# Reordering the result's stores, and two instructions late in the attention, in a two-layer encoder on one core

## The chip, the cores and the metric

The kernel runs on one core of a Trainium2 chip. The metric is the time of one execution on the device in microseconds (us); lower is better. A core has TensorE (PE, the matrix engine, with weight loads shown apart as PEld), VectorE (DVE), ScalarE (ACT), GpSimd (POOL) and SyncE (SP), each with its own stream of instructions that runs in order. They meet through semaphores. DMA engines move data between the chip's memory and the on-chip buffers; a transfer is issued by an instruction in the stream of SP, ACT or POOL, and such a stream is called that engine's queue here.

## The reference

One sequence of 512 tokens with 1024 features passes through two layers; all inputs are float32. Cut to what matters:

```python
def stick_breaking_attention(h, w_qkv, w_o):      # layer 0's mixer, 16 heads of 64
    ...
        z = jnp.einsum('bhqd,bhkd->bhqk', qb, kb).astype(jnp.float32) * scale
        mask = k_pos < q_pos
        log_keep = jnp.where(mask, jax.nn.log_sigmoid(-z), 0.0)
        after = lax.cumsum(log_keep, axis=3, reverse=True) - log_keep
        w = jnp.where(mask, jnp.exp(jax.nn.log_sigmoid(z) + after), 0.0)
        outs.append(jnp.einsum('bhqk,bhkd->bhqd', w.astype(vb.dtype), vb))
    ...
    return o @ w_o

def reference(...):
    for layer in range(DEPTH):                     # 2
        h = rms_norm(x, norm_mix[layer])
        y = stick_breaking_attention(...) if layer % 2 == 0 else rglru_block(...)
        x = x + y
        h = rms_norm(x, norm_mlp[layer])
        x = x + squared_relu_mlp(h, mlp_w1[layer], mlp_w2[layer])
    return rms_norm(x, norm_final)
```

The weight of a key for a query is sigmoid(z) times the product of sigmoid(-z) over the keys between the two. `rglru_block` is a gated linear recurrence over time, `squared_relu_mlp` is relu(h @ w1) squared, times w2, with 4096 inner features.

## The kernel before, in words

**Numbers in two halves.** A float32 operand is split into a rounded high half and the rest, the low half. ScalarE makes the high half (a cast), VectorE subtracts it for the low half, and a product is three matmuls: high x high, high x low, low x high (`three`, lines 234 to 238). Nearly all of the work of VectorE and ScalarE is this splitting. Weights come as slabs of 1024 x 128; `slab` (line 219) issues the load on SP's queue (line 223), casts the slab on ScalarE (line 229) and subtracts on VectorE (line 231), in one or more cuts. It takes its raw tile from a ring of 3 and its halves from rings of 4, so an early slab has to be used up before a later one is split.

**Who orders what.** TensorE's instructions run in the order in which the program emits them. For the other engines a planner simulates the program and picks, for each engine, the next instruction that is ready by its own clock, the earlier emitted one first, unless something holds it: `tc.issue_after(ins)` puts the instructions of a block behind `ins` on its engine, `tc.high_priority()` puts them first, and an `Ordered` wrapper (line 788) chains every instruction of one engine to the one before. An instruction that was emitted late can thus be planned early. What the planner chose is fixed; on the chip an engine whose next instruction isn't ready waits, and everything behind it waits too.

**The attention** (lines 303 to 770) works on 8 pairs of heads. A pair has a chain of 8 score steps (`score_steps`, line 586; 2 heads j times 4 query blocks qb of 128) and a chain of 18 value steps (`value_steps`, line 628). A score step multiplies queries and keys into one of two PSUM banks with the tag z (lines 595 and 596). ScalarE reads the bank twice: line 603 makes sigmoid(z) into `w`, line 604 sigmoid(-z) into `keep`; after the second read the bank is free. GpSimd masks the diagonal block (line 608), VectorE runs the product over the keys as a recurrence, `tensor_tensor_scan` (line 614), and GpSimd multiplies (line 618). A value step transposes the weights of one key block kb on TensorE (line 636) and splits the result (high half line 651, low half line 652), then multiplies it with the values (lines 662 and 663). For the last key block, kb = 3, the halves are 128 columns in tiles named `lasth` and `lastl`.

The chains are interleaved with filling matrix products by due times (constants SCORE0, PACE and so on), so that TensorE always has work. Late in the attention, the filling work is the output projection: `so_part` for output slabs 4 and 5, `so_steps` for slabs 0 to 3 (line 537), and `so_late`. Two chains overlap at that point: the scores of the last pair, 7 (PAIRS - 1), and the values of pair 6 (PAIRS - 2). The scores of pair 7, head 1, block 2 stand at about 202 us in TensorE's stream; the values of pair 6, head 1, kb = 3 at about 205 to 209 us.

**After the attention** come the residual with the first feed-forward layer, the recurrent block, and the second feed-forward layer. The feed-forward layers multiply blocks of matrices with fewer block products (`Mlp`, from line 795), and their last products go with the final normalization.

**The end** (function `end` inside the last `with`, lines 1847 to 1880) has the result in row tiles t = 0 to 3 of 128 tokens and halves h = 0, 1 of 512 features, so `(t, h)` is a store of 128 x 512, 256 KB. A tile is squared and summed on ScalarE; `root` (line 1815) makes 1/rms; the tile is multiplied by the norm's gain and by 1/rms. `both` (line 1827) does the two multiplications in one VectorE instruction (line 1831); `one` (line 1835) only multiplies by 1/rms, on ScalarE (line 1840) or, for the very last piece, on VectorE (line 1842), where GpSimd has multiplied by the gain before. Each ends with `store` (line 1821), which issues the transfer on SP's queue. In program order the stores are (0,0), (0,1), (1,0), (1,1), (2,1), (2,0), right half of (3,0), (3,1), left half of (3,0); the halves of (3,0) are 128 KB each. GpSimd's instructions in this function are held to program order by `EG = Ordered(G)` (line 1779); SP's aren't.

Of the kernel before, what the change touches and what calls it, by code (L numbers as in the profile page):

```python
# [15 lines left out]
ALU = mybir.AluOpType  # L16
# [3 lines left out]
S = 512  # L20
D = 1024
C = D // P
# [15 lines left out]
CUT = 2  # L38
# [26 lines left out]
def hybrid_encoder(  # L65
# [23 lines left out]
    nc = tc.nc  # L89
    V, A, G, PE = nc.vector, nc.scalar, nc.gpsimd, nc.tensor  # L90
# [16 lines left out]
    def f(ap):  # L107
        return ap.bitcast(F32)
# [107 lines left out]
    slabs, loads = count(), count()  # L216
    behind = [None]

    def slab(src, cut=1, ks=range(C), at=0):
        raws = rawpools[next(loads) % len(rawpools)]  # L220
        raw = raws.tile([P, C, P], F32, tag="raw", name="raw", bufs=3 if raws is wpool else 1)
        k = slice(ks.start, ks.stop)
        nc.sync.dma_start(out=raw[:, k, :], in_=src[:, k, :])
        pool = wpools[next(slabs) % len(wpools)]
        wh = half_slab(pool, "wh", at)
        wl = half_slab(pool, "wl", at)
        for i in range(cut):
            k = slice(ks.start + i * len(ks) // cut, ks.start + (i + 1) * len(ks) // cut)
            A.copy(wh[:, k, :], raw[:, k, :])  # L229
            with tc.issue_after(behind[0]) if behind[0] else nullcontext():  # L230
                V.tensor_tensor(wl[:, k, :], raw[:, k, :], f(wh[:, k, :]), ALU.subtract)  # L231
        return wh, wl
# [63 lines left out]
    NB = S // P  # L296
# [10 lines left out]
    with ExitStack() as actx:  # L307
# [228 lines left out]

        def so_steps(c, tag):

            wh, wl = slab(w_so[c], CUT)
            ps = bank(tag)  # L540
            so[c] = ps, wh, wl
            for k in range(C - 2):
                three(ps, bh[:, k, :], bl[:, k, :], wh[:, k, :], wl[:, k, :], k == 0, False)
                yield
# [42 lines left out]
        def score_steps(pair):  # L587

            for j in range(2):
                for qb in range(NB):  # L590
                    n = (qb + 1) * P
                    nn = max(n, 2 * P)
                    lhsT = q[pair][j][:, qb * P : n]
                    z = bank("z")
                    PE.matmul(z[:, :nn], lhsT, kh[pair][j][:, :nn], start=True, stop=False)
                    PE.matmul(z[:, :nn], lhsT, kl[pair][j][:, :nn], start=False, stop=True)
                    keep = home_tile("keep", 4, "keep")
                    pool = home if qb == NB - 1 else hp
                    wt = pool.tile([P, n], F32, tag=f"w{qb}", name=f"w{qb}", bufs=3)
                    if pair == 0:  # L600
                        V.tensor_tensor(keep[:, :n], z[:, :n], norm["r"][:, :n], ALU.mult)
                        z = keep
                    A.activation(wt, z[:, :n], AF.Sigmoid, scale=norm["rp"][:, qb : qb + 1])
                    marks["keep"] = A.activation(  # L604
                        keep[:, :n], z[:, :n], AF.Sigmoid, scale=norm["rn"][:, qb : qb + 1]
                    )
                    t = wt[:, qb * P : n]
                    G.affine_select(
                        t, t, pattern=[[-1, P]], compare_op=ALU.is_gt,
                        fill=0.0, base=0, channel_multiplier=1,  # L610
                    )
                    sc = scans[turns[0] % 3]
                    turns[0] += 1
                    V.tensor_tensor_scan(  # L614
                        sc[:, S - n : S][:, ::-1], keep[:, :n][:, ::-1], later[:, S - n :][:, ::-1],
                        1.0, ALU.mult, ALU.max,
                    )
                    G.tensor_tensor(wt, wt, sc[:, S - n + 1 : S + 1], ALU.mult)  # L618
                    w[pair, j, qb] = wt
                    yield  # L620

        lows = []

        def low():
            pair, o = lows.pop()
# [2 lines left out]
        def value_steps(pair):  # L628
# [3 lines left out]
            def turn(j, kb):  # L632
# [17 lines left out]
                with tc.high_priority():  # L650
                    A.copy(dh, tr[:, :n])
                    left[j, kb] = V.tensor_tensor(dl, tr[:, :n], f(dh), ALU.subtract)

            def times(j, kb):
                nonlocal o
# [1105 lines left out]
    with ExitStack() as mctx:  # L1761
# [14 lines left out]
            mlp.turns = count(4)  # L1776

        gb = []
        EG = Ordered(G)

        def factors():
            for h in range(2):
# [35 lines left out]
            V.reciprocal(rt, rt)  # L1818
            return rt

        def store(t, h, cols=slice(0, S)):
            nc.sync.dma_start(
                out=out[t * P : (t + 1) * P, h * S + cols.start : h * S + cols.stop],
                in_=mlp.y(t, h)[:, cols],
            )
# [6 lines left out]
            store(t, h, cols)  # L1832
            return done

        def one(t, h, rt, cols=slice(0, S), e=A, last=None):

            y = mlp.y(t, h)[:, cols]
            if e is A:
                with tc.issue_after(last.ins) if last else nullcontext():
                    A.activation(y, y, AF.Copy, scale=rt)  # L1840
            else:
                V.tensor_scalar(y, y, rt, None, ALU.mult)
            store(t, h, cols)

        def end(ws, xs):
            EG.turn(True)
            for t in range(2):
                square(t, 0, 0)
                scaled(t, 0)
# [26 lines left out]
            both(2, 0, two, last=mlp.gained)  # L1876
            rt = root(3, 2)
            both(3, 0, rt, parts[1])
            one(3, 1, rt)
            one(3, 0, rt, parts[0], V)  # L1880

        end.ready = factors
# [69 lines left out]
```

## Time and profile before

| what | us |
|---|---|
| median of 3 runs | 1023.08 (1023.04 to 1023.11) |
| the profiled execution's own time | 1023.33 |
| its span, first to last instruction | 1021.0 |
| TensorE busy | 1012.2 |
| VectorE busy | 862.2 |
| ScalarE busy | 710.9 |
| GpSimd busy | 178.3 |

The profile is of one execution. Times in its rows are in us from the span's start unless marked ns. A row of the timeline has the start, the duration, the engine, the line of the program, the operation, the tile written and those read, and the shapes; `x2` means that two instructions were merged into the row, and a bracket at the end is idle time before it and what ended it. Matmuls overlap: a row's duration is longer than the distance to the next start, so distances between starts are what counts. A row of the waits has the engine and tile that waited, what it waited for, the total, the number of times and the longest. A row of the windows view has the stretch, its length and the busy time of PE, PEld, DVE, ACT and POOL with the number of instructions in brackets, then the granted TensorE clock, the share of the DMA engines and GB/s. A row of the DMA view has the tiles, the queue, the count, the size of one and the median time in us from issue to landing.

### The profile page before, as it was taken

The page shows a single profiled execution, that of the slowest core. Times are in us where ns is not written, and L with a number is a line of the kernel's source. Part 1 is how long each engine was busy: PE and PEld are TensorE (multiplying, and loading weights), DVE is VectorE, ACT ScalarE, POOL GpSimd, SP SyncE. Part 2 cuts the span into 40 slices and gives each one's busy share as a digit, 9 for nine tenths or more (in the row PEclk, how much of TensorE's full clock was granted, in tenths as well). Part 3 has the DMA queues.
Part 4 walks back from the last instruction along what each step waited for, and adds up shares of the span by engine and source line. Part 5 has one row for each costly group of instructions (what it writes and reads, how often), then busy time and mean ns, then how long its engine had stood idle before and what let it go on. Part 6 is the DMA issues. An engine that isn't in the chain of part 4 may idle for free.

```text
span 1021.0 us, 16117 instructions
## 1 busy us (share of the span) xinstructions
PE 1012.2 (99%) x5954; PEld 892.3 (87%) x5954; DVE 862.2 (84%) x1157; ACT 710.9 (70%) x1109; POOL 178.3 (17%) x243
## 2 busy tenths in 40 slices
PE   9999999999999999999999999999999999999997
PEld 7988888888888988988988888888988988988986
DVE  7978787847789898898899888985998898898897
ACT  7777676835766873873875799966973873873875
POOL 0454344420000010010011121100020010010013
PEclk9999999999999999999999999999999999999999
DMA  7845454537536767667683576452367667667653
GB/s 239 232 110 148 119 150 101 154 106 269 153 82 197 180 150 196 172 149 198 166 225 83 139 186 170 104 200 89 88 143 203 171 143 202 180 138 201 168 122 104
DMA packets 53550, 161.53 MB, mean 158 GB/s; under 512 B 6752, under 2 KB 8288, under 8 KB 53472
## 3 DMA queue, kind: packets, MB, share of 16 engines
q1 hardware_dynamic: 42240, 120.48, 35.9%
q0 software_dynamic: 10944, 39.85, 22.8%
q8 instruction: 47, 0.77, 0.3%
q14 instruction: 31, 0.25, 0.1%
q10 hardware_dynamic: 288, 0.18, 0.1%
HBM read 138.46 MB, written 4.19 MB: 140 GB/s over the span
## 4 chain that ended last, share of the span: by engine, by line
PE 98%; DMA 0%; ACT 0%; DVE 0%; issue 0%; POOL 0%; SPq 0%; DVEq 0%; ACTq 0%
PE ps_t L1155 16%; PE ps_acc L1024 10%; PE ps_z L1024 9%; PE ps_acc L1155 9%; PE ps_o L1024 6%; PE ps_acc L236 5%; PE ps_acc L238 5%; PE ps_acc L237 5%; PE ps_z L1155 4%; PE ps_t L236 2%; PE ps_t L237 2%; PE ps_t L238 2%; PE ps_t L636 2%; PE ps_o L236 2%; PE ps_o L238 2%; PE ps_o L237 2%
## 5 line engine op out<-in xcount | busy, mean ns | idle before, releaser
L797 ACT CAST wh<-b 128x1024 fp32r<-128x1024 f32 x174 | 180.7, 1050 | 111.1 <-DVE b L797 74.1
L797 DVE TENSOR_TENSOR wl<-b,wh 128x1024 fp32r<-128x1024 f32 x174 | 210.7, 1221 | 42.9 <-ACT wh L797 41.7
L1100 POOL DMA_DIRECT2D b<-in_w_dn x40 | 35.0, 876 | 281.8 <-DVE b L797 191.6
L236 PE MATMUL ps_acc<-xgh,wh 128*128 128x512 f32 x192 | 78.3, 408 | 0.0
L238 PE MATMUL ps_acc<-xgl,wh 128*128 128x512 f32 x192 | 75.2, 392 | 0.0
L237 PE MATMUL ps_acc<-xgh,wl 128*128 128x512 f32 x192 | 75.1, 391 | 0.0
L1100 POOL DMA_DIRECT2D b<-in_w_up x26 | 22.6, 870 | 297.7 <-DMA b<-in_w_up 81.9
L614 DVE TENSOR_TENSOR_SCAN scan<-keep,later 128x128 f32<-128x128 f32 (+1 forms) x64 | 58.2, 912 | 16.6 <-ACT keep L604 13.3
L797 ACT ACTIVATE u<-u 128x512 f32<-128x512 f32 x103 | 65.0, 632 | 9.0 <-DVE u L797 7.2
L229 ACT CAST wh<-raw 128x512 fp32r<-128x512 f32 (+2 forms) x66 | 46.5, 742 | 26.7 <-issue 7.5
L231 DVE TENSOR_TENSOR wl<-raw,wh 128x512 fp32r<-128x512 f32 (+2 forms) x66 | 56.9, 890 | 7.5 <-ACT wh L229 7.4
L618 POOL TENSOR_TENSOR w<-w,scan 128x128 f32<-128x128 f32 (+1 forms) x64 | 53.5, 838 | 54.9 <-DVE scan L614 49.8
L797 DVE TENSOR_TENSOR b<-b,b 128x1024 f32<-128x1024 f32 x50 | 61.2, 1223 | 1.3
L797 DVE TENSOR_TENSOR u<-u 128x512 f32<-128x512 f32 (+1 forms) x85 | 54.4, 640 | 3.9 <-ACT u L797 2.5
L797 ACT CAST wh<-raw 128x1024 fp32r<-128x1024 f32 x47 | 49.0, 1048 | 5.8 <-PE ps_acc L1155 5.7
L1024 PE MATMUL ps_z<-xgh,wh 128*128 128x256 f32 x216 | 50.5, 277 | 0.0
L1155 PE MATMUL ps_t<-wh,sl 128*128 128x512 f32 x120 | 46.8, 390 | 0.0
L1155 PE MATMUL ps_t<-wh,bl 128*128 128x512 f32 x120 | 46.8, 390 | 0.0
L1155 PE MATMUL ps_t<-wh,bh 128*128 128x512 f32 x120 | 46.8, 390 | 0.0
L1155 PE MATMUL ps_t<-wh,sh 128*128 128x512 f32 x120 | 46.7, 389 | 0.0
L797 DVE TENSOR_TENSOR wl<-raw,wh 128x1024 fp32r<-128x1024 f32 x37 | 45.6, 1231 | 1.1 <-ACT wh L797 1.1
L1024 PE MATMUL ps_acc<-low,wh 128*128 128x256 f32 x192 | 44.7, 276 | 0.0
(431 smaller groups left out, 3207.9 us busy)
## 6 DMA issues: line engine op xcount, KB each, us to landing
b<-in_w_dn SPq DMA_DIRECT2D x48, 512.0 KB, 4.4
b<-in_w_dn POOLq DMA_DIRECT2D x40, 512.0 KB, 5.6
b<-in_w_up SPq DMA_DIRECT2D x39, 512.0 KB, 4.5
b<-in_w_up POOLq DMA_DIRECT2D x26, 512.0 KB, 5.3
raw<-in_w_dn SPq DMA_DIRECT2D x16, 512.0 KB, 4.6
raw<-in_w_in SPq DMA_DIRECT2D x16, 512.0 KB, 3.8
raw<-in_w_up SPq DMA_DIRECT2D x13, 512.0 KB, 3.8
raw<-in_w_qk SPq DMA_DIRECT2D x12, 512.0 KB, 3.8
```

Of the source, the lines that this page charges most:

```text
L229: A.copy(wh[:, k, :], raw[:, k, :])
L231: V.tensor_tensor(wl[:, k, :], raw[:, k, :], f(wh[:, k, :]), ALU.subtract)
L236: PE.matmul(ps, wh, ah, start=start, stop=False)
L237: PE.matmul(ps, wl, ah, start=False, stop=False)
L238: PE.matmul(ps, wh, al, start=False, stop=stop)
L614: V.tensor_tensor_scan(sc[:, S - n : S][:, ::-1], keep[:, :n][:, ::-1], later[:, S - n :][:, ::-1], 1.0, ALU.mult, ALU.max,)
L618: G.tensor_tensor(wt, wt, sc[:, S - n + 1 : S + 1], ALU.mult)
L636: PE.transpose(tr[:, (qb - kb) * P : (qb - kb + 1) * P], w[pair, j, qb][:, kb * P : (kb + 1) * P], ident,)
L797: ins = getattr(self.e, name)(*args, **kwargs)
L1024: PE.matmul(ps[:, i * HS : (i + 1) * HS], m, y, start=new and i == k == low == 0 and y is h, stop=(low, i, k) == steps[-1], skip_group_che ...
L1100: G.dma_start(out=unit[b].rearrange("p j n -> p (j n)"), in_=unit["src"](to), accum_op=ALU.add)
L1155: PE.matmul(sums[to][i], m, y[:, j, :], start=new and g == j == low == 0 and m is h, stop=g == low == j == 1, skip_group_check=not new,)
```

## The change

It has three parts. First, output slab 3's casts on ScalarE are put behind the second read of the scores of pair 7, head 1, block 1: `slab` gets a parameter `after`, `so_steps` passes it for c = 3, and line 604's instruction is remembered under its pair, head and block. Second, the recurrence of pair 7, head 1, block 3, the last of all, isn't issued by its score step; it is kept, with the GpSimd multiply that follows it, and issued by the value step of pair 6, head 1, kb = 3, behind that step's low half. Third, SP's stores at the end are held to program order by `ES = Ordered(nc.sync)`, and the store of (3,1) is issued from ScalarE's queue.

```diff
-    def slab(src, cut=1, ks=range(C), at=0):
+    def slab(src, cut=1, ks=range(C), at=0, after=None):
...
-            A.copy(wh[:, k, :], raw[:, k, :])
+            with tc.issue_after(after) if after else nullcontext():
+                A.copy(wh[:, k, :], raw[:, k, :])
...
         def so_steps(c, tag):
-            wh, wl = slab(w_so[c], CUT)
+            after = marks.get((PAIRS - 1, 1, 1)) if c == 3 else None
+            wh, wl = slab(w_so[c], CUT, after=after and after.ins)
...
-                    marks["keep"] = A.activation(
+                    marks["keep"] = marks[pair, j, qb] = A.activation(
...
-                    V.tensor_tensor_scan(
-                        sc[:, S - n : S][:, ::-1], keep[:, :n][:, ::-1], later[:, S - n :][:, ::-1],
-                        1.0, ALU.mult, ALU.max,
-                    )
-                    G.tensor_tensor(wt, wt, sc[:, S - n + 1 : S + 1], ALU.mult)
-                    w[pair, j, qb] = wt
+                    def rest(after=None, sc=sc, keep=keep, wt=wt, n=n, at=(pair, j, qb)):
+                        with tc.issue_after(after.ins) if after else nullcontext():
+                            V.tensor_tensor_scan(
+                                sc[:, S - n : S][:, ::-1], keep[:, :n][:, ::-1],
+                                later[:, S - n :][:, ::-1], 1.0, ALU.mult, ALU.max,
+                            )
+                        G.tensor_tensor(wt, wt, sc[:, S - n + 1 : S + 1], ALU.mult)
+                        w[at] = wt
+                    if (pair, j, qb) == (PAIRS - 1, 1, NB - 1):
+                        last_scan.append(rest)
+                    else:
+                        rest()
...
                     left[j, kb] = V.tensor_tensor(dl, tr[:, :n], f(dh), ALU.subtract)
+                if (pair, j, kb) == (PAIRS - 2, 1, NB - 1):
+                    last_scan.pop()(left[j, kb])
...
-        EG = Ordered(G)
+        EG, ES = Ordered(G), Ordered(nc.sync)
...
-        def store(t, h, cols=slice(0, S)):
-            nc.sync.dma_start(
+        def store(t, h, cols=slice(0, S), queue=ES):
+            queue.dma_start(
...
-            EG.turn(True)
+            for e in (EG, ES):
+                e.turn(True)
...
-            one(3, 1, rt)
+            one(3, 1, rt, queue=A)
             one(3, 0, rt, parts[0], V)
```

More of the change, by code (lines that the diff above doesn't have):

```diff
@@ L613, in score_steps @@
                     turns[0] += 1
-                    V.tensor_tensor_scan(
-                        sc[:, S - n : S][:, ::-1], keep[:, :n][:, ::-1], later[:, S - n :][:, ::-1],
-                        1.0, ALU.mult, ALU.max,
-                    )
-                    G.tensor_tensor(wt, wt, sc[:, S - n + 1 : S + 1], ALU.mult)
-                    w[pair, j, qb] = wt
+                    def rest(after=None, sc=sc, keep=keep, wt=wt, n=n, at=(pair, j, qb)):
[10 more added lines that the diff above has]
+                        rest()
                     yield
-        lows = []
+        lows, last_scan = [], []
         def low():
@@ L1833, in both, with one @@
             return done
-        def one(t, h, rt, cols=slice(0, S), e=A, last=None):
+        def one(t, h, rt, cols=slice(0, S), e=A, last=None, queue=ES):
             y = mlp.y(t, h)[:, cols]
@@ L1842, in one @@
                 V.tensor_scalar(y, y, rt, None, ALU.mult)
-            store(t, h, cols)
+            store(t, h, cols, queue)
         def end(ws, xs):
-            EG.turn(True)
+            for e in (EG, ES):
+                e.turn(True)
             for t in range(2):
```

## The prediction, made before the changed kernel ran

> **What bounds the kernel now.** I began with the chain that ended last and then looked at its end with the windows view.
>
> ```profile
> PE 98%; DMA 0%; ACT 0%; DVE 0%; issue 0%; POOL 0%; SPq 0%; DVEq 0%; ACTq 0%
> ```
> ```profile
> 1014.00:1021.00 7.00, 0.22 (x2) 0.01 (x1) 2.34 (x5) 2.32 (x6) 1.22 (x2) 0.75 0.49 184
> ```
>
> TensorE carries 98% of the chain. It stops near 1014.2, and the remaining 6.8 us of the span belong to the last normalization and the result's stores. So time can be won in two ways only: a gap in TensorE's stream closes, or the tail behind it gets shorter. The waits of the weight loads (TensorE's in-order front) between 199 and 210 us, late in the attention, show two gaps and nothing else:
>
> ```profile
> PEld ps_z L595 <- ACT keep L604: 0.5, 1, 0.5
> PEld ps_o L663 <- DVE lastl L652: 0.4, 1, 0.4
> ```
>
> These are durations of waits; what they cost is read from the starts of the matmuls, because a waiting weight load partly lies under the matmul before it. Start time is the first column:
>
> ```profile
> 201.72 0.39 PE L238 MATMUL ps_acc<-bl,wh 128*128 128x512 f32 x1
> 202.17 0.44 PE L595 MATMUL ps_z<-kh,q 128*128 128x384 f32 x1
> 202.45 0.34 PE L596 MATMUL ps_z<-kl,q 128*128 128x384 f32 x1
> 202.63 0.39 PE L236 MATMUL ps_acc<-bh,wh 128*128 128x512 f32 x1
> ```
> ```profile
> 207.45 0.40 PE L238 MATMUL ps_acc<-bl,wh 128*128 128x512 f32 x1
> 207.68 0.28 PE L662 MATMUL ps_o<-th,v 128*128 128x256 f32 x1
> 207.80 0.28 PE L663 MATMUL ps_o<-tl,v 128*128 128x256 f32 x1
> ```
> ```profile
> 208.61 0.27 PE L662 MATMUL ps_o<-lasth,v 128*128 128x256 f32 x1
> 209.00 0.39 PE L663 MATMUL ps_o<-lastl,v 128*128 128x256 f32 x1
> 209.22 0.39 PE L236 MATMUL ps_acc<-bh,wh 128*128 128x512 f32 x1
> ```
>
> Undisturbed, the next matmul starts 0.23 after one of 512 columns (207.45 to 207.68), 0.18 after 384 (202.45 to 202.63) and 0.12 after 256 (207.68 to 207.80). First gap: 202.17 - 201.72 = 0.45 instead of 0.23, and 202.45 - 202.17 = 0.28 instead of 0.18, together 0.32 us. Second gap: 209.00 - 208.61 = 0.39 instead of 0.12, and 0.22 instead of 0.12, together 0.37 us. The attention can give at most 0.69 us.
>
> **The change part by part: the slab's casts.** The scores of pair 7, head 1, query block 2 need a z bank that is free again once ScalarE has read block 0's scores for the second time (line 604). ScalarE's order:
>
> ```profile
> 199.97 1.14 ACT L229 CAST wh<-raw 128x512 fp32r<-128x512 f32 x2
> ```
> ```profile
> 201.75 0.37 ACT L604 ACTIVATE keep<-ps_z,rn 128x128 f32<-128x128 f32 x1
> ```
>
> That read ends at 202.12, 0.05 before the matmul starts at 202.17. The 1.14 us ahead of it are the two casts of output slab 3 (fourth slab pair, just free). Behind block 1's second read, as the change puts them, they no longer precede block 0's, which can end about 1.1 earlier, near 201.0; the matmul is due at 201.95 (201.72 + 0.23). The gap closes: -0.32. What the casts serve comes much later:
>
> ```profile
> 215.63 0.48 PE L236 MATMUL ps_z<-bh,wh 128*128 128x512 f32 x1
> 219.43 0.60 PE L636 MATMUL ps_t<-ident,w 128*128 128x128 f32 x4
> ```
>
> At 215.63 slab 3's products begin. Two casts and two subtracts later than 202 are covered by more than 10 us, so I cost the move at nothing. Two things move with the casts. The subtracts (line 231) cannot run before their cast, so VectorE does them among the scans instead. And the raw buffer comes free some 2 us later, so the SP queue's next weight load, and the x loads queued behind it, issue later; their data is used by the residual behind the attention, so this too costs nothing.
>
> **The recurrence.** VectorE at the second gap, with an earlier instruction of the same form as the first row ahead of it:
>
> ```profile
> 199.22 0.71 DVE L581 TENSOR_TENSOR kh<-raw,q 128x512 fp32r<-128x512 f32 x1
> ```
> ```profile
> 206.20 1.33 DVE L581 TENSOR_TENSOR kh<-raw,q 128x512 fp32r<-128x512 f32 x1
> 207.46 1.30 DVE L614 TENSOR_TENSOR_SCAN scan<-keep,later 128x512 f32<-128x512 f32 x1
> 208.69 0.26 DVE L652 TENSOR_TENSOR lastl<-ps_t,lasth 128x128 fp32r<-128x128 f32 x1
> ```
>
> The low half `lastl` ends at 208.95 and TensorE takes it at 209.00. Its inputs are older than the scan; it is only queued behind it. Swapped, it ends at 207.46 + 0.26 = 207.72, against 208.73 at which its matmul is due (208.61 + 0.12), or 208.41 once the first gap is gone: 0.69 to spare, gap closed, -0.37. The scan then ends near 209.0. Its GpSimd multiply follows it, and the first transpose that reads head 1's weights stands at 219.43 (row above): 10 us of cover. Nothing waits newly on TensorE; what is late next is again `lastl`, with that 0.69.
>
> A rule of the Trainium skill speaks against this. First the row: L581 took 0.71 at 199.22 and 1.33 at 206.20, on the same shape, the second time beside this GpSimd work:
>
> ```profile
> 206.94 0.74 POOL L608 TENSOR_SCALAR_AFFINE_SELECT w<-w 128x128 f32<-128x128 f32 x1
> ```
>
> So a VectorE subtract can lose 0.62 there. The Trainium skill, "SBUF — State Buffer", section "Who interferes with whom", says that a VectorE instruction with two SBUF inputs and a GpSimd instruction that reads SBUF exclude each other on a shared port; the trace agrees with the stretched row. Slab 3's moved subtracts are of that kind; this is a rival below.
>
> **The tail.** SP issues the stores in the order that the planner chose, and a store that waits holds those behind it. What makes the last five ready, then SP's issues (2 in a row where it says x2), then the size and landing of the last one:
>
> ```profile
> 1014.22 0.71 ACT L1840 ACTIVATE c<-c,rt 128x512 f32<-128x512 f32 x1
> 1014.66 1.11 DVE L1831 SCALAR_TENSOR_TENSOR c<-c,rt,gb 128x512 f32<-128x512 f32 x1
> 1015.88 0.48 DVE L1831 SCALAR_TENSOR_TENSOR c<-c,rt,gb 128x256 f32<-128x256 f32 x1
> 1015.94 0.72 ACT L1840 ACTIVATE c<-c,rt 128x512 f32<-128x512 f32 x1 [0.29 <-DVE rt L1818]
> 1016.28 0.35 DVE L1842 TENSOR_SCALAR c<-c,rt 128x256 f32<-128x256 f32 x1
> ```
> ```profile
> 1015.79 0.33 SPq L1822 DMA_DIRECT2D out<-c  x1
> 1016.22 0.89 SPq L1822 DMA_DIRECT2D out<-c  x2
> 1017.20 0.91 SPq L1822 DMA_DIRECT2D out<-c  x2
> ```
> ```profile
> out<-c SPq DMA_DIRECT2D x1, 128.0 KB, 2.1
> ```
> ```profile
> DMA packets 716, 1.05 MB, mean 381 GB/s; under 512 B 77, under 2 KB 332, under 8 KB 716
> ```
>
> Row-tile 2's right half is ready at 1014.93 (14.22 + 0.71), yet SP issues nothing until 1015.79, just as the left half is done (14.66 + 1.11 = 15.77): SP waited for the left half first. From there on five stores queue at a pitch of about 0.49, the last from 1017.70 (18.11 less its 0.41), landing 2.1 later at 1019.80; the span ends 1.2 after that. The last line covers 1016.60 to 1019.35, in which the 1.05 MB of all five (three of 128x512 f32, two of 128x256) move without a pause.
>
> With the queue held to program order the right half goes out near 1014.95, the left at 1015.79, the first 128 KB (15.88 + 0.48) at 1016.4, and the last 128 KB, ready at 1016.63, one pitch later at 1016.9. The other 256 KB, ready at 1016.66, go out from ScalarE's queue at 1016.7, ScalarE having nothing behind it. By issues, the last landing is 1016.9 + 2.1 = 1019.0: -0.8. By bytes, one 0.26 MB store has left the burst: 0.79 MB at 381 GB/s from 1016.6 end at 1018.7, not 1019.35: -0.65. I take -0.75. The trace has no store on ScalarE's queue; its nearest row, and SP's of the same size at the same moment at the kernel's start:
>
> ```profile
> raw<-in_w_qk SPq DMA_DIRECT2D x7, 128.0 KB, 4.3
> raw<-in_w_qk ACTq DMA_DIRECT2D x1, 128.0 KB, 4.0
> ```
>
> So its landing lies between 2.1 (SP's store at this place) and 4.0. Since SP's own loads took as long at the start, I take 2.1; a gain from the second queue is excluded by bytes that already move without a pause.
>
> The Trainium skill, "DMA: Bandwidth & Descriptors", section "Specifications", gives about 358 GB/s as one core's HBM limit; by it the 0.79 MB would end at 1018.8 and the sum below would be 0.1 smaller in its gain. The 381 GB/s row is above it, so the row decides.
>
> **The sum.** -0.32 - 0.37 - 0.75 = -1.44. The profiled execution took 1023.33 (span 1021.0 and 2.3 around it), 0.25 over the median of 1023.08, so 1021.9 for such an execution and **1021.6** for the median. All rows are of one execution, and TensorE has no other gap here, so a shift of its stream passes on whole to the tail.
>
> **The rivals.**
> 1. *VectorE falls behind, `lastl` is late again* (the port rule as a mechanism). Two subtracts stretched by 0.62 each make 1.24; `lastl` then ends at 208.96 against 208.41, a gap of 0.55 + 0.1 for the restart. Gain 1.44 - 0.65 = 0.8: 1022.3. It decides from 0.69 of delay. Against it: the subtracts only change places, and VectorE's total stays. 0.12.
> 2. *The mark or the order does nothing.* The casts are held only if block 1's read was emitted before slab 3 is asked for. TensorE runs in emitted order, and even the next block's scores (202.17) precede slab 3's products (215.63) by far, so the mark exists. If one attention move had no effect: 1021.9 to 1022.0. 0.04.
> 3. *ScalarE's queue lands late* (the slower side). If its store takes 4.0 as at the start, it lands at 16.7 + 4.0 = 1020.7 instead of 1019.8: the tail loses 0.9, the attention gives 0.69, sum +0.2: 1023.3. It costs the tail's gain from 3.1 and makes the kernel slower from 3.8. 0.05.
> 4. *A new order in the residual.* Nothing holds VectorE's and ScalarE's order by hand there, and the planner may order anew:
>
> ```profile
> 242.18 1.22 DVE L231 TENSOR_TENSOR wl<-raw,wh 128x1024 fp32r<-128x1024 f32 x1
> ```
> ```profile
> 245.13 0.39 PE L237 MATMUL ps_o<-xgh,wl 128*128 128x512 f32 x1
> ```
>
> The second up-projection slab's low half ends at 243.40 and is used at 245.13: 1.73 to spare. Three more operations of 1.22 ahead of it would cost 1.9: 1023.5. One wouldn't cost anything. 0.05.
>
> **How the numbers follow.** Forecast 0.74. The range of the forecast itself runs from -1.76 (gaps closed, and the last landing 2.0 after 1016.7) to -1.1, that is 1021.3 to 1022.0; down to 1021.0 for a tail a little better than my bounds, and up to 1022.8 it takes in rivals 1 and 2 and half the way to 3. 0.2% is 2.05 us, about what a measurement of this kernel can tell from no change: every case but a stray one stays within it. Faster 0.05 (more than the listed gaps and the tail's bound would be needed), same 0.90, slower 0.05.
>
> **What would show it.** Both waits quoted above gone from the list of weight-load waits; L595 starting 0.23 after the matmul before it, L663 0.12 after L662; slab 3's casts after 202; the scan behind `lastl`; the right half's store issued near 0.8 us before the left's; one store on ScalarE's queue; the last landing 0.7 to 0.8 nearer to TensorE's end. I am wrong if a new wait appears between 210 and 270, if `lastl` still waits, or if the last store lands more than 3 us after its issue.

## The result, and the profile after

Over 19 timed runs of each kernel the changed one takes 1021.78 us (median), the one before 1023.35: a ratio of 0.9986, with a 95% interval of 0.998 to 0.9993. The forecast was 1021.6, in a range from 1021.0 to 1022.8, and a change of less than 0.2%; all three hold. The profiled execution of the changed kernel took 1021.84 with a span of 1019.7, against 1023.33 and 1021.0: 1.49 and 1.3 less.

The waits of TensorE's weight loads between 30 and 1014 us (total, times, longest) are what a reader should look at first. The two waits of the attention are gone, and no other has taken their place; what is left are two short ones in the second feed-forward layer, between 820 and 850 us, and these stood there before the change too.

```profile
PEld ps_t L1167 <- DVE sl L809: 0.3, 1, 0.3
PEld ps_acc L1167 <- ACT sh L809: 0.3, 1, 0.3
```

The timeline of TensorE around the two places and at its end (start, us; line numbers in the attention are 1 to 12 higher than before):

```profile
201.69 0.40 PE L239 MATMUL ps_acc<-bl,wh 128*128 128x512 f32 x1
201.92 0.34 PE L597 MATMUL ps_z<-kh,q 128*128 128x384 f32 x1
202.09 0.34 PE L598 MATMUL ps_z<-kl,q 128*128 128x384 f32 x1
202.27 0.40 PE L237 MATMUL ps_acc<-bh,wh 128*128 128x512 f32 x1
...
208.29 0.27 PE L674 MATMUL ps_o<-lasth,v 128*128 128x256 f32 x1
208.40 0.28 PE L675 MATMUL ps_o<-lastl,v 128*128 128x256 f32 x1
208.52 0.40 PE L237 MATMUL ps_acc<-bh,wh 128*128 128x512 f32 x1
...
1013.27 0.28 PE L1130 MATMUL ps_t<-wh,sl 128*128 128x256 f32 x1
```

The starts are 0.23, 0.17 and 0.18 apart at the first place, 0.11 and 0.12 at the second: TensorE runs through. Against the execution before, this place was reached 0.03 earlier (201.69 against 201.72) and left 0.70 earlier (208.52 against 209.22); the last matmul starts at 1013.28 (the row has 1013.27; group starts are rounded) against 1013.94, so 0.66 is kept to the end: 0.03 from the earlier start and 0.63 won behind it.

ScalarE shows the moved casts behind the read they used to delay, VectorE the moved subtracts and, at last, `lastl` ahead of the recurrence. First ScalarE, then VectorE:

```profile
198.13 1.14 ACT L582 CAST q<-raw 128x512 fp32r<-128x512 f32 x2 [0.87 <-DMA raw<-in_w_so]
...
200.40 0.38 ACT L606 ACTIVATE keep<-ps_z,rn 128x128 f32<-128x128 f32 x1
...
201.36 1.17 ACT L230 CAST wh<-raw 128x512 fp32r<-128x512 f32 x2
```
```profile
202.40 1.76 DVE L232 TENSOR_TENSOR wl<-raw,wh 128x512 fp32r<-128x512 f32 x2
...
206.93 0.27 DVE L662 TENSOR_TENSOR lastl<-ps_t,lasth 128x128 fp32r<-128x128 f32 x1
207.12 1.35 DVE L619 TENSOR_TENSOR_SCAN scan<-keep,later 128x512 f32<-128x512 f32 x1
```

Block 0's second read ends at 200.78, 1.14 ahead of its matmul. `lastl` ends at 207.20, with 1.2 to spare to 208.40. The bracket in the first row becomes important below: ScalarE stood still for 0.87 until a load had landed.

The tail, SP's and ScalarE's queues by issue, then the landings of the last two stores (KB each, us from issue to landing):

```profile
1014.28 0.33 SPq L809 DMA_DIRECT2D out<-c  x1
1015.12 0.33 SPq L809 DMA_DIRECT2D out<-c  x1
1015.72 0.83 SPq L809 DMA_DIRECT2D out<-c  x2
1016.02 0.38 ACTq L1834 DMA_DIRECT2D out<-c  x1
1016.15 0.41 SPq L809 DMA_DIRECT2D out<-c  x1
```
```profile
out<-c ACTq DMA_DIRECT2D x1, 256.0 KB, 2.1
out<-c SPq DMA_DIRECT2D x1, 128.0 KB, 2.3
```

Row-tile 2's right half now goes out 0.84 before its left half, and the last store at 1016.15 (the third row overlaps it, because it spans two issues). It lands near 1018.4 (issue and landing time are rounded in the rows), 5.15 behind TensorE's last start, against 5.81 before (1019.75 less 1013.94).

In both executions 1.27 us of the span follow the last landing. So the span's 1.3 are 0.63 in the attention, 0.66 in the tail and the 0.03 by which this execution was ahead already.

### The profile page after: what moved, and what is told of

It is laid out like the page before. It is cut to its first block, busy times and chain, and to the rows that moved or that the text cites. A ratio compares the mean times of both kernels' runs of the same rounds, so it can differ in the third digit from the quotient of the medians.

```text
span 1019.7 us, 16115 instructions
## 1 busy us (share of the span) xinstructions
PE 1012.2 (99%) x5954; PEld 893.3 (88%) x5954; DVE 862.5 (85%) x1157; ACT 710.4 (70%) x1109; POOL 178.2 (17%) x243
## 4 chain that ended last, share of the span: by engine, by line
PE 99%; DMA 0%; DVE 0%; ACT 0%; SPq 0%; issue 0%; ACTq 0%
PE ps_t L1167 16%; PE ps_acc L1036 10%; PE ps_z L1036 9%; PE ps_acc L1167 9%; PE ps_o L1036 6%; PE ps_acc L237 5%; PE ps_acc L239 5%; PE ps_acc L238 5%; PE ps_z L1167 4%; PE ps_t L237 2%; PE ps_t L239 2%; PE ps_t L238 2%; PE ps_t L646 2%; PE ps_o L237 2%; PE ps_o L239 2%; PE ps_o L238 2%
```

## The experiments

My theory was the prediction's: the two gaps have separate causes and close one by one, and the tail gains by the order and by the second queue together. Rivals: the gaps are one budget, so that closing the first only widens the second; the tail's gain comes from one of its two parts alone; and the gaps have another cause than the named instructions.

Every kernel below but the last was timed in 11 runs, against 27 to 33 of the kernel before on the same chip. These ratios can't tell most of the parts from no change. The traces can, if TensorE's length is measured from a fixed matmul that no edit touches: the low-half product just ahead of the first gap. That matmul itself starts at another time in each execution. Two rows of TensorE's timeline, the earliest (the kernel labelled f2_all_slab6) and the latest (e2_scan):

```profile
201.12 0.40 PE L239 MATMUL ps_acc<-bl,wh 128*128 128x512 f32 x1
```
```profile
202.14 0.40 PE L239 MATMUL ps_acc<-bl,wh 128*128 128x512 f32 x1
```

1.0 us of spread has arisen before the change's first place is reached, so spans alone would mislead. All executions, by their own rows. "Length" goes from that matmul to the start of the last one; "tail" from there to the last landing; the gaps are what the start-to-start times have over those of the changed kernel, good to about 0.02:

| kernel | start | length | gaps 1, 2 | tail | ScalarE's wait for slab 6's load | median / before | ratio (95%) |
|---|---|---|---|---|---|---|---|
| before | 201.72 | 812.22 | 0.32, 0.37 | 5.81 | 1.12 | | |
| changed | 201.69 | 811.59 | 0, 0 | 5.15 | 0.87 | 1021.78 / 1023.35 | 0.9986 (0.998 to 0.9993) |
| e1_casts | 201.48 | 812.32 | 0, 0.74 | 5.82 | 1.05 | 1022.67 / 1023.21 | 0.9998 (0.9989 to 1.0007) |
| e2_scan | 202.14 | 811.91 | 0, 0 | 5.82 | 0.65 | 1022.91 / 1023.21 | 0.9998 (0.999 to 1.0007) |
| e3_stores | 201.43 | 812.04 | 0.18, 0.37 | 5.17 | 0.98 | 1022.26 / 1023.21 | 0.9994 (0.9985 to 1.0002) |
| e4_order | 201.45 | 811.82 | 0, 0.25 | 5.30 | 0.78 | 1022.44 / 1023.21 | 0.9996 (0.9987 to 1.0005) |
| e5_actq | 201.76 | 811.92 | 0.07, 0.34 | 5.82 | 0.89 | 1022.87 / 1023.0 | 0.9999 (0.999 to 1.0008) |
| e9_att | 201.92 | 811.54 | 0, 0 | 5.81 | 0.94 | 1022.66 / 1023.0 | 0.9996 (0.9987 to 1.0005) |
| e8_slab6 | 201.72 | 811.54 | 0, 0 | 5.81 | none | 1022.65 / 1023.0 | 0.9996 (0.9988 to 1.0005) |
| e7_split | 201.48 | 811.55 | 0, 0 | 5.62 | 0.76 | 1022.32 / 1023.0 | 0.9993 (0.9984 to 1.0002) |
| f1_slab6_stores | 201.65 | 811.59 | 0, 0 | 5.18 | none | 1021.91 / 1023.08 | 0.9989 (0.998 to 0.9998) |
| f2_all_slab6 | 201.12 | 811.59 | 0, 0 | 5.16 | none | 1021.86 / 1023.08 | 0.9987 (0.9978 to 0.9996) |
| f3_again | 201.66 | 811.59 | 0, 0 | 5.17 | 1.00 | 1021.84 / 1023.08 | 0.9988 (0.9979 to 0.9997) |
| f4_casts_again | 201.93 | 812.49 | 0, 0.73 | 5.82 | 1.29 | one run: 1023.74 | |

Without gaps the length is 811.54 to 811.59 in seven executions; e2_scan is the one exception, and it has a reason of its own. The edits below are relative to the changed kernel.

**e1_casts: the casts' move alone.**

```diff
-                    if (pair, j, qb) == (PAIRS - 1, 1, NB - 1):
+                    if False:
...
-                if (pair, j, kb) == (PAIRS - 2, 1, NB - 1):
+                if False:
...
-            for e in (EG, ES):
-                e.turn(True)
+            EG.turn(True)
...
-            one(3, 1, rt, queue=A)
+            one(3, 1, rt)
```

> Only slab 3's casts are held behind the second read of block 1's scores; recurrence and stores as before. Three theories. Each gap for itself: the first gap (0.32 us) closes, the second (0.37) stays, time -0.3. VectorE's clock is fixed: lastl still ends at 208.95 while TensorE now comes 0.32 earlier, so the second gap grows to 0.65 and the time stays the same. VectorE moves up too: in the changed kernel it stood free for the low half at 206.93, half a microsecond earlier than before, because the stretched subtract of 1.33 took 0.66 there; scan 1.24 and low half 0.26 behind that end at 208.43, so the second gap shrinks to about 0.1 to 0.2 and the time falls by 0.5 to 0.6.

The first gap is gone, and the second has taken all of it. The weight-load wait (before: 0.4), TensorE's and VectorE's timelines:

```profile
PEld ps_o L675 <- DVE lastl L662: 0.8, 1, 0.8
```
```profile
208.12 0.28 PE L674 MATMUL ps_o<-lasth,v 128*128 128x256 f32 x1
208.87 0.39 PE L675 MATMUL ps_o<-lastl,v 128*128 128x256 f32 x1 [0.47 <-DVE lastl L662]
```
```profile
206.16 0.66 DVE L583 TENSOR_TENSOR kh<-raw,q 128x512 fp32r<-128x512 f32 x1
...
207.08 1.55 DVE L619 TENSOR_TENSOR_SCAN scan<-keep,later 128x512 f32<-128x512 f32 x1
208.55 0.26 DVE L662 TENSOR_TENSOR lastl<-ps_t,lasth 128x128 fp32r<-128x128 f32 x1
```

Counted from the reference matmul, TensorE comes to the value matmul 0.25 earlier (6.64 behind it instead of 6.89), but VectorE's stretch ahead of `lastl` hasn't moved with it: `lastl` ends 7.33 behind it, and 7.23 before. 0.69 of gap became 0.74, as the second of the three theories had it. The two gaps aren't separate terms: the first gave TensorE a rest that the second would otherwise have needed.

**e2_scan: the recurrence's move alone.**

```diff
-            after = marks.get((PAIRS - 1, 1, 1)) if c == 3 else None
+            after = None
...
-            for e in (EG, ES):
-                e.turn(True)
+            EG.turn(True)
...
-            one(3, 1, rt, queue=A)
+            one(3, 1, rt)
```

> Only the last recurrence is issued behind the low half; casts and stores as before. My theory: lastl ends near 207.7, the second gap (0.37 us) closes, the first (0.32) stays, time -0.37. Rival: it was the stretched subtract of 1.33 ahead of both that made the low half late; then a wait at L663's weight load of 0.1 to 0.4 stays.

No gap was left at either place, though slab 3's casts stood where they always had. ScalarE's row in this execution:

```profile
198.38 1.14 ACT L582 CAST q<-raw 128x512 fp32r<-128x512 f32 x2 [0.65 <-DMA raw<-in_w_so]
```

and the same row before the change:

```profile
198.44 1.14 ACT L580 CAST q<-raw 128x512 fp32r<-128x512 f32 x2 [1.12 <-DMA raw<-in_w_so]
```

These are output slab 6's casts. ScalarE waits there for that slab's load, 0.65 this time and 1.12 in the execution that I had predicted from. That gives another theory: what makes the read late is this wait, and slab 3's casts only stand between. It also means that this run doesn't show what the recurrence's move alone does when the load lands late. (The 0.32 by which its length is over 811.59 lies elsewhere: TensorE waited 0.5 between 760 and 780 us for a cast in the second feed-forward layer, which the waits of the changed kernel and of e1_casts, e3_stores, e4_order, e5_actq, e7_split and e8_slab6 do not show. Its cause stays open.)

**e3_stores: the stores' part alone.**

```diff
-            after = marks.get((PAIRS - 1, 1, 1)) if c == 3 else None
+            after = None
...
-                    if (pair, j, qb) == (PAIRS - 1, 1, NB - 1):
+                    if False:
...
-                if (pair, j, kb) == (PAIRS - 2, 1, NB - 1):
+                if False:
```

> Only the stores: SP held to program order and the store of (3,1) on ScalarE's queue; attention as before, with both of its gaps. My theory: the last landing comes 0.65 to 0.75 nearer to TensorE's end and the time falls by as much. Rival: the tail's gain came from the attention's shift, and the time stays the same.

The tail is 5.17 against 5.81, the changed kernel's gain (0.64 of its 0.66). The attention, untouched, has its two gaps, but the first is smaller than before: 0.18 with a wait for slab 6's load of 0.98.

**e4_order: SP's order alone,** e3_stores and

```diff
-            one(3, 1, rt, queue=A)
+            one(3, 1, rt)
```

> Only SP's program order; all nine stores on SP, attention as before. If bytes alone bound the tail: 0.79 MB from 1016.6, as in the kernel with both, -0.65. If issues bound it: the stores go out at 1014.95, 1015.79, 1016.4, 1016.9 and 1017.4, the last lands 2.1 later at 1019.5 instead of 1019.8, -0.3.

The tail is 5.30, so the order carries 0.51 of the 0.66; it came out between its two bounds. SP issues the right half at once here too (one row holds all five issues):

```profile
1014.27 2.79 SPq L809 DMA_DIRECT2D out<-c  x5
```

All five stores are issued by SP here, and their bytes pause. Between 1017.00 and 1017.25 they move at 295 GB/s, in the changed kernel, whose TensorE ends at the same time (1013.27), at 418 (first this kernel, then the changed one; the last number of a row):

```profile
1017.00:1017.25 0.25, 0.00 (x0) 0.00 (x0) 0.00 (x0) 0.00 (x0) 0.00 (x0) 0.50 0.76 295
```
```profile
1017.00:1017.25 0.25, 0.00 (x0) 0.00 (x0) 0.00 (x0) 0.00 (x0) 0.00 (x0) 0.50 1.09 418
```

The attention is as it was before the change, but the first gap is 0 and the wait for the load 0.78.

**e5_actq: ScalarE's queue alone, SP in the planner's order,** e3_stores and

```diff
-            for e in (EG, ES):
-                e.turn(True)
+            EG.turn(True)
```

> Only the store of (3,1) on ScalarE's queue; SP keeps the planner's order, in which the left half of tile 2 holds back its right half; attention as before. If bytes bound the tail: 1.05 MB still start at 1016.6, the distance from TensorE's last start to the last landing stays near 5.8 us, no gain. If the pitch of SP's issues bounds it: one store fewer on SP, distance 5.3, -0.5.

The tail is 5.82: nothing gained. ScalarE's store lands 2.6 after its issue, SP's last two (2 in the row) 2.7 after theirs, and the same 1.05 MB move in one burst (1016.2 to 1019.1, its slow start included):

```profile
out<-c ACTq DMA_DIRECT2D x1, 256.0 KB, 2.6
out<-c SPq DMA_DIRECT2D x2, 128.0 KB, 2.7
```
```profile
DMA packets 717, 1.05 MB, mean 361 GB/s; under 512 B 78, under 2 KB 333, under 8 KB 717
```

Here an earlier issue on a second queue was turned into a longer landing, because the same bytes start together. Only once the order has taken a store out of the burst, and the rest pauses (e4_order), does the second queue give its 0.13 (5.30 to 5.17).

**e9_att: both attention moves, the stores as before.**

```diff
-            for e in (EG, ES):
-                e.turn(True)
+            EG.turn(True)
...
-            one(3, 1, rt, queue=A)
+            one(3, 1, rt)
```

> Casts and recurrence as changed, stores as before. The two moves alone gave no measurable gain: in the run with the casts alone the second gap grew to 0.74, which is as much as both gaps before. My theory now: the two are one chain, the low half is late by VectorE's clock, so a gain needs both. Both gaps closed, -0.3 to -0.7, and the tail's distance 5.8 as before. Rival: the attention's part of the gain is an accident of one execution and a gap stays.

No gap at either place with a wait for the load of 0.94, and a length of 811.54. The length falls by 0.68 against the execution before; by the medians it is 0.34 (1022.66 against 1023.0), and the ratio's interval includes 1, no change.

**e8_slab6: neither move, but slab 6's casts held behind block 1's read,** so that the read no longer stands behind their load. Both moves and the stores are undone as above, and in `late_slab`:

```diff
-                A.copy(h, raw[:, a:b, :])
+                after = marks[PAIRS - 1, 1, 1].ins if c == 6 else None
+                with tc.issue_after(after) if after else nullcontext():
+                    A.copy(h, raw[:, a:b, :])
```

> Neither of the change's moves; instead the two casts of output slab 6, needed near 229, are held behind the second read of block 1's scores. Theory: what made the first gap is ScalarE waiting for slab 6's load to land before those casts (its cast began 1.31, 1.46, 1.69 and 1.79 us before the same matmul in four executions with slab 3's casts in the old place, and a gap of 0.22 and 0.07 came with the two latest, none with the others). Without that wait block 0's second read ends near 201.6 at the latest and the first gap is gone; the second gap stays (0.4 to 0.7), as VectorE's order of recurrence and low half is unchanged. Time between -0.3 and +0.1. Rival: slab 3's casts are what holds the reads; then the first gap of 0.1 to 0.3 is still there.

ScalarE and VectorE in this kernel (line numbers 2 higher than in the changed one):

```profile
198.14 1.14 ACT L230 CAST wh<-raw 128x512 fp32r<-128x512 f32 x2
...
199.92 0.38 ACT L608 ACTIVATE keep<-ps_z,rn 128x128 f32<-128x128 f32 x1
...
200.97 1.14 ACT L584 CAST q<-raw 128x512 fp32r<-128x512 f32 x2
```
```profile
206.47 1.20 DVE L621 TENSOR_TENSOR_SCAN scan<-keep,later 128x512 f32<-128x512 f32 x1
207.60 0.26 DVE L664 TENSOR_TENSOR lastl<-ps_t,lasth 128x128 fp32r<-128x128 f32 x1
```

Slab 3's casts still stand ahead of block 0's read, and it ends at 200.30, earlier than in the changed kernel (200.78). So those casts alone do no harm. (The read came 1.82 earlier than before, more than the wait of 1.12: the hold also takes slab 6's casts from ahead of it. That it is the wait which counts is shown by the runs in which the order is the same and only the landing differs; they are set side by side under f4_casts_again.) And what I had not expected: the second gap closes as well, with the recurrence still ahead of `lastl`. VectorE, whose work follows ScalarE's casts and reads, begins the recurrence at 206.47 instead of 207.46, and `lastl` ends at 207.86, 0.57 before its matmul (208.43). So one hold, on the casts that wait for the load, closes both gaps, and the change goes around that wait twice.

**e7_split: a try at a still shorter tail.** Row-tile 2's left half is multiplied and stored in two pieces, the first ahead of the last collected product:

```diff
+            ahead = None
...
-                mlp.collect("P4", 1, ps, cols)
+                with tc.issue_after(ahead.ins) if ahead else nullcontext():
+                    mlp.collect("P4", 1, ps, cols)
...
                 if i == 0:
+                    ahead = both(2, 0, two, parts[0], last=mlp.gained)
                     one(2, 1, two, last=sq)
...
-            both(2, 0, two, last=mlp.gained)
+            both(2, 0, two, parts[1], last=mlp.gained)
```

> The whole change, and the left half of tile 2 multiplied and stored in two pieces, the first in VectorE's idle time ahead of the last collected product. If bytes bound the tail: 0.13 MB less in the burst behind TensorE, last landing 0.2 to 0.3 earlier than with the change, distance 4.9 instead of 5.15. If the last stores' readiness bounds it: 5.15 again. If the first piece delays the last collected product (GpSimd multiplies beside it), the distance grows by up to 0.3.

The tail became longer, 5.62 against 5.15. VectorE and, for the same time, GpSimd:

```profile
1012.79 1.11 DVE L1843 SCALAR_TENSOR_TENSOR c<-c,rt,gb 128x256 f32<-128x256 f32 x1
1013.83 0.47 DVE L809 SCALAR_TENSOR_TENSOR c<-ps_t,rr,c 128x256 f32<-128x256 f32 x1
1014.22 0.55 DVE L1843 SCALAR_TENSOR_TENSOR c<-c,rt,gb 128x256 f32<-128x256 f32 x1
```
```profile
1012.34 2.15 POOL L809 TENSOR_TENSOR c<-c,gb 128x512 f32<-128x512 f32 x2
```

The first piece, which reads two SBUF tiles, took 1.11 beside GpSimd's two multiplies, where the same line and shape takes 0.48 alone (1015.88 in the execution before). The last collected product, queued behind it on VectorE, waited until 1013.83 and delayed everything that follows it: the third of the outcomes foreseen, at 0.47 instead of up to 0.3. The Trainium skill, "SBUF — State Buffer", section "Who interferes with whom", says that a VectorE instruction with two inputs in SBUF contends with a GpSimd instruction that reads SBUF; the row of 1.11 agrees.

**f1_slab6_stores, f2_all_slab6, f3_again: is there a better version?** The hold of e8_slab6 with the changed stores and without the two moves (f1), the whole change with that hold (f2), and the changed kernel once more as their yardstick (f3). The edit of f1:

```diff
-            after = marks.get((PAIRS - 1, 1, 1)) if c == 3 else None
+            after = None
...
+                after = marks[PAIRS - 1, 1, 1].ins if c == 6 else None
+                with tc.issue_after(after) if after else nullcontext():
+                    A.copy(h, raw[:, a:b, :])
...
-                    if (pair, j, qb) == (PAIRS - 1, 1, NB - 1):
+                    if False:
...
-                if (pair, j, kb) == (PAIRS - 2, 1, NB - 1):
+                if False:
```

f2 has only the three lines with `c == 6` of it; f3 has no edit.

> Slab 6's casts held behind block 1's second read, and the stores as changed; slab 3's casts and the last recurrence in their old places. If slab 6's load was the common cause of both gaps: no gap, tail distance 5.15, as fast as the whole change (within 0.3 us), -1.0 to -1.5 against the kernel before. Rival: without the change's own moves a gap of 0.2 or more comes back.

> The whole change and slab 6's casts held as well. If the whole change has closed both gaps whatever the landing, this adds nothing: the same time as the change within 0.3 us. If in some executions of the change the landing still opens a gap, this one is faster on the median by 0.1 to 0.3.

> The changed kernel itself once more, beside the two others on the same chip: -1.2 to -1.6 against the kernel before; no gap in the attention, tail distance 5.15.

1021.91, 1021.86 and 1021.84, and the same length of 811.59 in all three. In these executions the hold replaces both moves, and with them it adds nothing. f2's span of 1019.1 against 1019.7 looks like a gain, but its reference matmul started 0.54 earlier (201.12 against 201.66), before the first instruction that the edit moves.

**f4_casts_again: e1_casts once more, one execution,** in the hope of an earlier landing, to see whether the second gap then shrinks as well.

> The casts of slab 3 alone once more, for a second landing of slab 6's load. If the low half's lateness follows that landing: slab 6's cast 1.5 to 1.8 before the reference matmul gives a second gap of 0.1 to 0.5, less than the 0.74 that came with 1.15. If VectorE's order alone sets it: 0.7 again whatever the landing.

The landing was the latest of all instead: a wait for the load of 1.29. The gap at `lastl` is 0.73 again, but another 0.22 has opened at an earlier value matmul, and the length is 812.49, the longest of all. That answers the question from the other end, once the landing is counted from the reference matmul. (The text above counts its 1.15 and 1.5 to 1.8 from a score matmul that starts 1.97 ahead of it, at 199.51 in e1_casts.) These are the six executions with slab 6's casts and the last recurrence in their old places; the stretch goes from the reference matmul to the one behind the second gap and is 6.83 in every execution without a gap:

| kernel | slab 6's casts start ahead of the reference | stretch | over 6.83 |
|---|---|---|---|
| e4_order | 3.65 | 7.12 | 0.29 |
| e5_actq | 3.53 | 7.25 | 0.42 |
| e3_stores | 3.42 | 7.35 | 0.52 |
| before | 3.28 | 7.50 | 0.67 |
| e1_casts | 3.12 | 7.61 | 0.78 |
| f4_casts_again | 2.96 | 7.77 | 0.94 |

The first and the last number add up to 3.94 or 3.95 in the first four and to 3.90 in the two with slab 3's casts moved. What the two gaps cost together follows the landing one for one, and the casts' move by itself takes 0.05 off it. By the same line, an estimate, e2_scan (3.76) would have had 0.19 left; with the recurrence moved it had nothing.

## Why the prediction was right, and where it was not

The three parts of the forecast gain came out as planned, and in that sense it was right: both gaps closed, and the last store landed earlier. Two steps inside it were wrong, the cause given for the first gap and the adding up of the two.

**The first gap: -0.32.** Its size in that execution was right and it closed. The step that failed is its cause, "The 1.14 us ahead of it are the two casts of output slab 3". They are one part of it; a wait for slab 6's load and that slab's own casts stand ahead of them. In the five executions with those casts in their old place and slab 6's unheld, the gap follows ScalarE's wait for slab 6's load one by one: 1.12 gives 0.32, 0.98 gives 0.18, 0.89 gives 0.07, and 0.78 and 0.65 give none. So the gap is the wait less about 0.8, and either pair of casts ahead of the read may be moved (e1_casts, e8_slab6). The row for it was in the trace that I had: the chain ScalarE's read, the casts ahead of it, and ahead of those a wait for a DMA. I stopped one step short.

**The second gap: -0.37.** It closes as predicted when the recurrence moves, and `lastl` had more to spare than I said (1.2 instead of 0.69), for two reasons that the runs don't separate: the load landed earlier here (slab 6's casts start 3.56 ahead of the reference, 3.28 before), and VectorE's last subtract of slab 6 took 0.66, and 1.33 before. The landing has its part: in e2_scan the subtract still took 1.33, the casts started 3.76 ahead, and `lastl` had 1.19 to spare. The failed step here is the adding up: "the attention can give at most 0.69 us" was right as a sum for that execution, but its two terms can't be taken one by one. With the casts' move alone nothing is gained (e1_casts: 0.74 for 0.69). What the recurrence's move alone gives when the load lands late, no run shows.

**-0.69 is one execution's price.** The execution profiled before had a late landing (1.12), and its stretch was 0.67 too long. The others with the attention as before have 0.52 (e3_stores), 0.42 (e5_actq) and 0.29 (e4_order). The attention part is worth 0.3 to 0.7, depending on how the load lands. The change also makes the landing matter less: with both moves there is no gap at waits from 0.76 to 1.00 (e7_split, the changed kernel, e9_att, f3_again). No execution of it had a later landing.

**The tail: -0.75.** Measured -0.66. I gave two bounds, -0.8 by issues and -0.65 by bytes, and took a value between them; the bound by bytes was the answer, and the sign "0.7 to 0.8 nearer" was missed by a little. The issues came as worked out (16.15 against 16.2, once the attention's gain is taken off), and the landing became longer instead, 2.3 for 2.1. That the second queue gives nothing by itself "by bytes that already move without a pause" was shown (e5_actq). What the prediction didn't see is that with the order alone the bytes do pause (e4_order): the order gives 0.51, the queue behind it 0.13 to 0.15. In the changed kernel they move without a pause from 1016.2 to 1017.9:

```profile
DMA packets 490, 0.67 MB, mean 393 GB/s; under 512 B 48, under 2 KB 280, under 8 KB 490
```

The Trainium skill, "DMA: Bandwidth & Descriptors", section "Specifications", gives about 358 GB/s as one core's HBM limit, a memory stack's 716 divided by its two cores; with one core running, this row is above it, as the row of before was (381).

**The rivals.** VectorE falling behind: the mechanism was there, the two moved subtracts took 0.71 and 1.12, but they end long before `lastl` is due. (The GpSimd row that the prediction quotes for the stretched subtract, at 206.94, lies beside its second half; beside its start lies a GpSimd multiply, shown below.) That the move does nothing, a late landing on ScalarE's queue (2.1), and a new order in the residual (the engines' orders are the same there) didn't come about.

**The sum.** -1.44 forecast, -1.29 shown by the two executions' rows (0.63 and 0.66), -1.57 by the medians, whose interval is -2.0 to -0.7; f3_again, the same kernel beside other runs of the kernel before, has -1.24. No row accounts for the rest of the -1.57. The 0.25 by which I took the profiled execution to lie over the median wasn't there: of three runs the median was 1023.08, of 19 it is 1023.35. From that the forecast would have been 1021.9. So 1021.6 owes its nearness to 1021.78 in part to luck: it started from a median 0.27 too low and took off 0.13 too little. (The far end of its range, -1.76, is -1.79 by the terms given for it, 0.69 and 1019.8 less 1018.7; nothing hangs on that.)

## What to carry to other kernels

When an instruction comes late, follow its engine's order back past the instruction just ahead of it to the last idle time: here that was a cast waiting for a load whose first matmul stood 30 us further on (229.24 in the execution before), and holding that slab's casts did what two moves did. Before two gaps are added up, ask whether the first gives the rest that the second would have to take; the test is to close one alone. In a tail of stores count first the bytes that start together: here an order that lets one store go earlier was worth 0.51, and a second queue 0.13 behind it and nothing without it.

## What the runs showed of the hardware that I had not expected

The same 512 KB load at the same place landed 3.5 to 4.2 us after its issue from one execution to the next, and in the six executions set side by side above that went with 0.3 to 0.9 us of TensorE's time.

A VectorE subtract and a GpSimd multiply that each read two on-chip tiles slowed one another, and the one that began later paid. Before the change, with the subtract of the prediction (206.20, 1.33) beside it, and then in the changed kernel, GpSimd ahead of VectorE:

```profile
206.12 0.87 POOL L618 TENSOR_TENSOR w<-w,scan 128x384 f32<-128x384 f32 x1 [1.32 <-DVE scan L614]
```
```profile
206.24 1.16 POOL L623 TENSOR_TENSOR w<-w,scan 128x384 f32<-128x384 f32 x1 [1.75 <-DVE scan L619]
206.01 0.66 DVE L583 TENSOR_TENSOR kh<-raw,q 128x512 fp32r<-128x512 f32 x1
```

Every execution in which the two overlap goes one of these two ways: 1.33 for the subtract when GpSimd began first, 0.66 when VectorE did.

The start of the kernel varies even more: the reference matmul at 202 us started anywhere between 201.12 and 202.14, in kernels whose instructions stand in the same order up to about 198 us. In the first 10 us TensorE was busy for 8.88 in f2_all_slab6 and 8.50 in e2_scan (the windows view; the first number of each triple is the engine's busy time, TensorE's first):

```profile
0.00:10.00 10.00, 8.88 (x61) 7.81 (x62) 5.06 (x14) 6.03 (x11) 2.07 (x15) 1.00 0.79 259
```
```profile
0.00:10.00 10.00, 8.50 (x57) 6.78 (x58) 4.63 (x14) 5.60 (x10) 2.07 (x15) 1.00 0.74 225
```

The loads moved 259 GB/s in the one and 225 in the other over that time. So the spread of this kernel, 1022.1 to 1024.2 over the 19 runs of before (one at 2568 aside), probably comes in part from how its first loads land; no run here tests that. The first three runs, 0.07 apart, gave no idea of the spread.
